# One core, two chained transformer blocks in split float32: the SBUF layout is moved so that the dense operands start at multiples of 512 bytes

## The chip, the core and the metric

The kernel runs on one core of a Trainium2 chip, in one launch. The metric is the device time of one execution in microseconds (us). Engines are named as in the profile: PE is TensorE's matrix product, PEld its weight load, DVE is VectorE, ACT is ScalarE, POOL is GpSimd, SP issues the weight DMAs. [...]

## The reference, cut to what matters

Two blocks run one after the other on 512 tokens of width 1024. Everything is float32.

```python
# block 1
h = rms_norm(x, g_pre_mix) * (1 + sc1) + sh1;  proj = h @ w_in
x = x + gt1 * rms_norm(concat(nsa_attention(...), dsa_attention(...)) @ w_out, g_post_mix)
h = rms_norm(x, g_pre_ffn) * (1 + sc2) + sh2
x = x + gt2 * rms_norm(square(relu(h @ w_up)) @ w_down, g_post_ffn)        # width 4096
# block 2
x = x + 0.5 * swiglu(rms_norm_2(x, norm_ffn1), gate, up, down)              # width 2816
p = rms_norm_2(x, norm_mix) @ w_in                                          # width 3328
x = x + concat(stick_breaking_attention(...), rwkv7_time_mix(...)) @ w_out
x = x + 0.5 * swiglu(rms_norm_2(x, norm_ffn2), gate, up, down)
```

## The kernel before

Activations lie transposed: 128 features on the partitions, 512 tokens (2048 bytes) along the row. A dense product is done in three float32r matrix products: each operand is split into a high part (float32r, rounded) and a low part (the rest), and high x high, low x high and high x low are summed in PSUM (`dense`, three calls of `mm`, whose one line is L339). The weights are the stationary operand, 128x128 (a row of 512 bytes), the activation is the moving operand, 128x512.

In the profile's rows `whi` and `wlo` are the two parts of the weights. The activations are named by what they hold: `hh`, `hl` are the normalized input of a block (pool `hp`, a pool on the right side of SBUF); `oh`, `ol` the attention's output (four tile pairs in pool `gp`, four in `hp`); `uh`, `ul` the squared ReLU in block 1's feed-forward; `vh`, `vl` the gated product in block 2's two SwiGLUs. Up products go to PSUM banks `ps_mm` (and the first ones of a SwiGLU to `ps_s`), down products to `ps_s`, so a row `ps_s<-uh,whi` is one matmul of block 1's down product.

`Stream` loads the weights: SP issues loads of 1 MB into two buffers `w32` (shown as `w`), ACT writes `whi` (L243), DVE writes `wlo` (L249), 1024 columns at a time, which is the weight of 24 matmuls. PE executes in the order in which the program lists its instructions. In the feed-forwards this order is plain: per output tile 24 matmuls over eight input tiles, one after the other. In block 2's mixer (`mix2`) the dense matmuls are fillers, listed by `weave` between the short products of the recurrence and of the attention (`ps_c`, `ps_pt`).

Where a tile lies in SBUF follows from the pools alone. Pools are stacked, from the left and from the right, and each tile takes the length of its row, rounded up to 32 bytes. So a small tile shifts all that comes behind it. In the program as built, before the change, the small constants of pool `cst` end at byte 18880 of a partition, which is 448 past a multiple of 512; `w32`, `whi`, `wlo`, the temporaries and most pools behind them start at 448 past such a multiple. In block 1's feed-forward the tile `g1` of 32 bytes lies ahead of `uh` and `ul` and moves them to 480. The right side ends 32 bytes short of a multiple of 512, which puts all tiles of `hp` at 480. `gp` happens to lie at 0.

Of the kernel before, what the change touches and what calls it, by code (L numbers as in the profile page):

```python
# [9 lines left out]
F32 = mybir.dt.float32  # L10
# [283 lines left out]
class K:  # L294
# [306 lines left out]
    def setup(self, es):  # L601
# [38 lines left out]
        cp = self.ces.enter_context(tc.tile_pool(name="cst1", bufs=1, side="right"))  # L640
# [19 lines left out]
        nc.vector.tensor_copy(cz[:, :, 0:1], self.vec("c", 0, 8).unsqueeze(2))  # L660
        self.cz = cz
        self.modc = cp.tile([128, 48], F32, name="modc")
        self.gs = cp.tile([128, 8], F32, name="gs")
        wap = self.xin.enter_context(tc.tile_pool(name="wap", bufs=1))
        self.wq = self.xin.enter_context(tc.tile_pool(name="wq", bufs=4))
        self.ada0 = deque()
# [54 lines left out]

    def open_h(self):
        self.hes = ExitStack()
        self.hp = self.hes.enter_context(self.tc.tile_pool(name="hp", bufs=8, side="right"))

    def ada_part(self, cg, bank="s"):
# [170 lines left out]
    def block1_attn(self):  # L897
# [219 lines left out]
        for i in (1, 2, 3):  # L1117
            w = work[:, WOFF[i] + 128 * i:WOFF[i] + 128 * i + 128]
            P.affine_select(out=w, in_=w, pattern=[[-1, 128]], compare_op=OP.is_ge, fill=FILL, base=0,
                            channel_multiplier=1)  # L1120
        m8 = self.ap.tile([128, 3, 8], F32, name="m8")
        dmask = self.ap.tile([128, 1152], BF, name="dmask")
        top = deque()

# [132 lines left out]
    def block1_ffn(self, oT):  # L1257
# [7 lines left out]
        es = ExitStack()  # L1265
        fp = es.enter_context(tc.tile_pool(name="fp", bufs=1))
        y = [fp.tile([128, T], F32, name=f"y{k}") for k in range(8)]
        g1 = fp.tile([128, 8], F32, name="g1")
        V.tensor_tensor(g1, self.modc[:, 16:24], self.vec("g_post_mix", 0, 8), op=OP.mult)
        self.gain("g_pre_ffn", 32)  # L1270

# [31 lines left out]
        for k in range(8):  # L1303
            t, t2 = (fp.tile([128, T], F32, name=n, tag=n, bufs=XB) for n in ("xr", "xg"))
# [492 lines left out]
    def rw_solve(self, f, u, ag):  # L1797
# [4 lines left out]
        t2 = self.rt  # L1802
# [14 lines left out]
        for half in (0, 1):  # L1817
# [9 lines left out]
            S.activation(w(ee), pv[:, :, 1], AF.Exp)  # L1827
            for _ in range(3):
                self.after("S", 256)
        dec = t2("dec", 8)  # L1830
        V.tensor_copy(dec, ch(ei)[:, :, 63])
        yield x

# [218 lines left out]
```

## Time and profile before

| | |
|---|---|
| median of three runs | 2000.85 us (1999.77 to 2000.95) |
| profiled execution, its own time | 2004.94 us |
| its span, first to last instruction | 2003.1 us |
[...]
| PE busy | 1926.2 us (96%), 11492 instructions recorded |
| DVE, ACT, POOL busy | 1079.5, 782.2, 147.8 us |
| read from HBM | 167.67 MB |

The profiled execution is 4.1 us (0.2%) above the median of the runs. Matmuls are pipelined: the duration in a row is from the first operand to the modelled end of the last result, and consecutive matmuls overlap. What a matmul costs in a stream is the distance from its start to the next start, so the rows to read are starts and counts, not durations. Some matmul records are missing from a trace.

### The profile page before, as it was taken

The page shows a single profiled execution, that of the slowest core. Times are in us where ns is not written, and L with a number is a line of the kernel's source. Part 1 is how long each engine was busy: PE and PEld are TensorE (multiplying, and loading weights), DVE is VectorE, ACT ScalarE, POOL GpSimd, SP SyncE. Part 2 cuts the span into 40 slices and gives each one's busy share as a digit, 9 for nine tenths or more (in the row PEclk, how much of TensorE's full clock was granted, in tenths as well). Part 3 has the DMA queues.
Part 4 walks back from the last instruction along what each step waited for, and adds up shares of the span by engine and source line. Part 5 has one row for each costly group of instructions (what it writes and reads, how often), then busy time and mean ns, then how long its engine had stood idle before and what let it go on. Part 6 is the DMA issues. An engine that isn't in the chain of part 4 may idle for free.

```text
span 2003.1 us, 27567 instructions
## 1 busy us (share of the span) xinstructions
PE 1926.2 (96%) x11492; PEld 1475.2 (74%) x11492; DVE 1079.5 (54%) x1798; ACT 782.2 (39%) x1353; POOL 147.8 (7%) x117
## 2 busy tenths in 40 slices
PE   5889999889999998999999999999999999999999
PEld 2766666668888886888888877677667778888887
DVE  6588875662434346543434555565657674444343
ACT  3666776442323233322222453322335652222221
POOL 3340110130000002000000000000002200000000
PEclk8999999889999998999999999999999899999999
DMA  7124123312322221223232321110101022323222
GB/s 292 56 98 143 65 87 135 106 63 84 105 84 100 90 94 61 98 84 105 85 105 85 105 92 44 43 44 23 38 18 33 1 105 84 106 85 105 87 98 90
DMA packets 27342, 171.54 MB, mean 86 GB/s; under 512 B 3153, under 2 KB 3409, under 8 KB 9041
## 3 DMA queue, kind: packets, MB, share of 16 engines
q1 hardware_dynamic: 23472, 163.44, 23.4%
q10 hardware_dynamic: 3744, 6.34, 0.9%
q8 instruction: 90, 1.47, 0.3%
q14 instruction: 36, 0.29, 0.0%
HBM read 167.67 MB, written 2.10 MB: 85 GB/s over the span
## 4 chain that ended last, share of the span: by engine, by line
PE 80%; ACT 2%; DVE 2%; POOL 1%; issue 1%; DMA 0%; ACTq 0%; POOLq 0%; DVEq 0%
PE ps_mm L339 45%; PE ps_s L339 22%; PE ps_c L339 7%; PE ps_pt L339 4%; PE ps_o L339 1%; POOL xr L1308 0%; PE ps_pt L878 0%; ACT whi L243 0%; POOL x L1357 0%; DMA x<-in_x 0%; DVE wlo L249 0%; PE ps_mm L734 0%; DVE hl L1372 0%; DVE y L1356 0%; POOL hl L1315 0%
## 5 line engine op out<-in xcount | busy, mean ns | idle before, releaser
L243 ACT ACTIVATE whi<-w 128x1024 fp32r<-128x1024 f32 (+4 forms) x277 | 274.7, 994 | 787.0 <-PE ps_mm L339 481.5
L339 PE MATMUL ps_mm<-hh,whi 128*128 128x512 f32 x1304 | 528.7, 406 | 21.7 <-ACT whi L243 9.3
L339 PE MATMUL ps_mm<-hh,wlo 128*128 128x512 f32 x1304 | 528.7, 406 | 6.1 <-DVE wlo L249 6.1
L339 PE MATMUL ps_mm<-hl,whi 128*128 128x512 f32 x1304 | 529.6, 406 | 2.9 <-DVE hl L1315 1.2
L249 DVE TENSOR_TENSOR wlo<-w,whi 128x1024 fp32r<-128x1024 f32 (+7 forms) x316 | 325.2, 1036 | 155.8 <-ACT whi L243 155.4
L339 PEld LDWEIGHTS ps_mm<-hh,whi 128*128 128x128 f32 x1304 | 248.2, 191 | 89.5 <-ACT whi L243 12.6
L339 PEld LDWEIGHTS ps_mm<-hh,wlo 128*128 128x128 f32 x1304 | 248.3, 190 | 74.7 <-DVE wlo L249 9.6
L339 PEld LDWEIGHTS ps_mm<-hl,whi 128*128 128x128 f32 x1304 | 248.1, 190 | 68.2 <-issue 4.5
L339 PE MATMUL ps_s<-vl,whi 128*128 128x512 f32 x352 | 137.2, 390 | 0.0
L339 PE MATMUL ps_s<-vh,wlo 128*128 128x512 f32 x352 | 137.0, 389 | 0.0
L339 PE MATMUL ps_s<-vh,whi 128*128 128x512 f32 x352 | 136.7, 389 | 0.0
L1413 DVE TENSOR_TENSOR su<-ps_mm,rr 128x512 f32<-128x512 f32 x42 | 29.0, 691 | 139.9 <-PE ps_mm L339 139.9
L1425 DVE SCALAR_TENSOR_TENSOR x<-ps_s,x 128x512 f32<-128x512 f32 x48 | 33.2, 692 | 129.4 <-PE ps_s L339 129.4
L339 PE MATMUL ps_s<-uh,whi 128*128 128x512 f32 x256 | 101.1, 395 | 0.0
L339 PE MATMUL ps_s<-ul,whi 128*128 128x512 f32 x256 | 101.1, 395 | 0.0
L339 PE MATMUL ps_s<-uh,wlo 128*128 128x512 f32 x256 | 101.1, 395 | 0.0
L1412 DVE TENSOR_TENSOR sg<-ps_mm,rr 128x512 f32<-128x512 f32 x42 | 29.1, 692 | 103.9 <-PE ps_mm L339 99.6
L339 PEld LDWEIGHTS ps_s<-vl,whi 128*128 128x128 f32 x352 | 66.1, 188 | 14.4 <-DVE vl L759 0.6
L339 PEld LDWEIGHTS ps_s<-vh,wlo 128*128 128x128 f32 x352 | 66.1, 188 | 13.9
L339 PEld LDWEIGHTS ps_s<-vh,whi 128*128 128x128 f32 x352 | 66.1, 188 | 13.8
L339 PEld LDWEIGHTS ps_s<-ul,whi 128*128 128x128 f32 x256 | 48.0, 187 | 11.8
L339 PEld LDWEIGHTS ps_s<-uh,whi 128*128 128x128 f32 x256 | 48.0, 187 | 11.7
(559 smaller groups left out, 2723.1 us busy)
## 6 DMA issues: line engine op xcount, KB each, us to landing
w<-in_gu SPq DMA_DIRECT2D x44, 1024.0 KB, 4.9
w<-in_win SPq DMA_DIRECT2D x17, 1024.0 KB, 5.0
w<-in_wada SPq DMA_DIRECT2D x16, 1024.0 KB, 5.4
w<-in_wup SPq DMA_DIRECT2D x16, 1024.0 KB, 4.8
w<-in_wdn SPq DMA_DIRECT2D x16, 1024.0 KB, 4.8
w<-in_dn SPq DMA_DIRECT2D x16, 1024.0 KB, 4.8
wa<-in_wada SPq DMA_DIRECT2D x8, 1024.0 KB, 13.4
w<-in_dn SPq DMA_DIRECT2D x8, 768.0 KB, 4.4
```

What stands on the lines that cost most here:

```text
L243: self.nc.scalar.activation(hi[:, :n], src, AF.Copy)
L249: self.nc.vector.tensor_tensor(lo[:, o:m], src[:, o:m], hi[:, o:m], op=OP.subtract)
L339: self.last_pe = self.nc.tensor.matmul(o, l, r, start=start, stop=stop, skip_group_check=True)
L1412: V.tensor_tensor(g, pg, r, op=OP.mult)
L1413: V.tensor_tensor(v, pu, r, op=OP.mult)
L1425: V.scalar_tensor_tensor(self.x[m], ps, 0.5, self.x[m], op0=OP.mult, op1=OP.add)
```

## The change

No instruction, no operand's shape and no order is changed; the built programs agree instruction by instruction on each engine, waits included, apart from the addresses (and the row length of three of the resized tiles). Five small edits resize or move small tiles, or add one that nothing uses.

```diff
@@ setup
-        self.gs = cp.tile([128, 8], F32, name="gs")
+        self.gs = cp.tile([128, 16], F32, name="gs")[:, :8]
@@ open_h
         self.hes = ExitStack()
+        self.hes.enter_context(self.tc.tile_pool(name="pad", bufs=1, side="right")).tile([128, 120], F32, name="pad")
         self.hp = self.hes.enter_context(self.tc.tile_pool(name="hp", bufs=8, side="right"))
@@ block1_attn
-        m8 = self.ap.tile([128, 3, 8], F32, name="m8")
+        m8 = self.ap.tile([128, 4, 8], F32, name="m8")[:, :3]
@@ block1_ffn
-        g1 = fp.tile([128, 8], F32, name="g1")
+        g1 = fp.tile([128, 128], F32, name="g1")[:, :8]
@@ rw_solve
-        dec = t2("dec", 8)
+        dec = self.small("dec", 8)
```

`dec` goes from the recurrence's pool to pool `cst`, which then ends at byte 18944 = 37 x 512; `pad` (480 bytes) fills the right end of SBUF; `g1` takes 512 bytes instead of 32. Start addresses modulo 512 bytes, and how many matmuls with 512 moving columns read them, counted in the built programs:

| operand | role | before | after | matmuls |
|---|---|---|---|---|
| `hh`, `hl` | moving | 480 | 0 | 4056 |
| `uh`, `ul` | moving | 480 | 0 | 768 |
| `oh`, `ol` in `hp` | moving | 480 | 0 | 96 |
| `oh`, `ol` in `gp` | moving | 0 | 0 | 96 |
| `vh`, `vl` | moving | 448 | 0 | 1056 |
| `whi`, `wlo` | weights of all of these | 448 | 0 | 6072 |

Other operands of PE move as well, by other amounts: the attention's `qst`, `kda`, `ksa` from 448 to 0, `kwa` from 384 to 448, `sbtri` and `negones` from 320 to 384, `P` and `PT` from 224 to 320; the token projection, where `whi` is the moving operand of 348 columns, reads half of its slices at 368 instead of 304.

## Rows read from the trace of the kernel before

**Rows 1.** The page: busy time, and the chain's shares by engine and line.

```profile
PE 1926.2 (96%) x11492; PEld 1475.2 (74%) x11492; DVE 1079.5 (54%) x1798; ACT 782.2 (39%) x1353; POOL 147.8 (7%) x117
...
PE 80%; ACT 2%; DVE 2%; POOL 1%; issue 1%; DMA 0%; ACTq 0%; POOLq 0%; DVEq 0%
```

**Rows 2.** Stretches: PE, PEld, DVE, ACT, POOL busy (instructions), granted clock, DMA share, GB/s.

```profile
32.00:120.00 88.00, 78.38 (x355) 61.37 (x355) 54.66 (x78) 51.16 (x85) 38.51 (x28) 0.90 0.21 72
120.00:320.00 200.00, 194.34 (x1199) 131.51 (x1198) 160.53 (x434) 144.43 (x366) 32.27 (x27) 1.00 0.32 111
...
425.00:769.00 344.00, 343.56 (x1473) 275.63 (x1471) 133.66 (x152) 106.39 (x137) 1.41 (x1) 1.00 0.28 95
...
876.00:1153.00 277.00, 277.00 (x1203) 225.14 (x1202) 124.08 (x147) 80.37 (x96) 0.00 (x0) 1.00 0.28 95
1153.00:1370.00 217.00, 215.36 (x2425) 155.61 (x2425) 123.73 (x244) 80.71 (x160) 0.00 (x0) 1.00 0.15 51
1370.00:1534.00 164.00, 157.94 (x1963) 112.50 (x1960) 101.02 (x206) 61.74 (x128) 3.31 (x3) 0.98 0.09 29
```

**Rows 3.** The chain that ended last, in order of time: start, length, what, count.

```profile
419.73 35.24 PE ps_mm L339 x140
454.97 44.80 PE ps_s L339 x192
499.77 44.80 PE ps_mm L339 x192
...
723.77 44.58 PE ps_s L339 x191
...
809.55 67.20 PE ps_mm L339 x288
876.75 43.55 PE ps_s L339 x192
920.30 89.60 PE ps_mm L339 x384
1009.90 43.56 PE ps_s L339 x192
...
1120.66 32.87 PE ps_s L339 x144
```

**Rows 4.** Order of time, PE, in the output projection: start, duration, instruction.

```profile
355.37 0.39 PE L339 MATMUL ps_mm<-oh,whi 128*128 128x512 f32 x1
...
358.12 0.40 PE L339 MATMUL ps_mm<-oh,whi 128*128 128x512 f32 x1
...
360.91 0.39 PE L339 MATMUL ps_mm<-oh,whi 128*128 128x512 f32 x1
```

**Rows 5.** Order of time, PE, at half clock, at the first feed-forward's start.

```profile
420.32 0.63 PE L339 MATMUL ps_mm<-hh,whi 128*128 128x512 f32 x1
420.75 0.63 PE L339 MATMUL ps_mm<-hl,whi 128*128 128x512 f32 x1
...
424.59 0.52 PE L339 MATMUL ps_mm<-hl,whi 128*128 128x512 f32 x1
```

**Rows 6.** The chain in order of time, in block 2's mixer.

```profile
1223.38 1.08 PE ps_c L339 x32
1224.46 1.13 PE ps_mm L339 x4
1225.59 1.08 PE ps_c L339 x32
```

**Rows 7.** Groups of instructions from 425 to 769 us: weight conversion on DVE and ACT.

```profile
L249 DVE TENSOR_TENSOR wlo<-w,whi 128x1024 fp32r<-128x1024 f32 x62 | 77.0, 1243 | 115.3 <-ACT whi L243 115.3
L243 ACT ACTIVATE whi<-w 128x1024 fp32r<-128x1024 f32 x62 | 65.8, 1061 | 202.3 <-PE ps_s L339 115.9 <-PE ps_mm L339 74.3 <-issue 12.0
```

**Rows 8.** The page: weight loads, KB each, median us from issue to landing.

```profile
w<-in_gu SPq DMA_DIRECT2D x44, 1024.0 KB, 4.9
```

**Rows 9.** Who waited for whom on PEld, 1153 to 1600 us: total, times, longest.

```profile
PEld ps_c L339 <- DVE tmt L1930: 11.4, 25, 1.6
PEld ps_c L339 <- DVE z L1921: 4.9, 11, 1.0
```

## The prediction

> **What bounds the kernel now.** I read the page first: PE is busy for 96% of the span and is 80% of the chain that ended last, DVE for 54% of the span, and DMA shows 0% of the chain [rows 1]. The stretches then show where PE leaves nothing free. From 425 to 769 us (block 1's feed-forward) it is busy for 343.56 of 344 us, from 876 to 1153 us (first SwiGLU) for all 277, in the mixer for 215.36 of 217 and 157.94 of 164; only the first 120 us have real gaps [rows 2]. So a matmul that ends sooner is worth its whole gain in nearly all of the span, if the next one can start sooner.
>
> The chain in order of time shows what one costs, because there the pieces are long unbroken runs. In the feed-forward a run of 192 takes 44.80 us, whether `ps_mm` (moving `hh`, `hl`) or `ps_s` (moving `uh`, `ul`). In the SwiGLU the same 192 take 43.55 or 43.56 us when they are the down product, with moving `vh`, `vl`; the up products there take 89.60 for 384, which is 44.80 for 192 again [rows 3]. So starts lie 44.80 / 192 = 233.3 ns apart in one kind and 43.56 / 192 = 226.9 ns in the other, same shape, same weights' tiles, same clock of 1.0. The kinds differ in one thing that I can name: `hh`, `hl`, `uh`, `ul` start at 480 past a multiple of 512, `vh`, `vl` at 448. The kind of product is not it, for `u` and `v` are both down products and differ, `u` and `h` are different products and agree.
>
> The output projection says the same inside one stage: its first four tile pairs lie at 0, its last four at 480. From 355.37 to 358.12 us twelve matmuls with tiles at 0 pass, 229.2 ns each; from 358.12 to 360.91 us twelve at 480, 232.5 ns each [rows 4]. The other rows that matter are those at the half clock: from 420.32 to 424.59 us ten starts, 427 ns apart, with operands at 480 [rows 5]. Halved that is 213.5 ns, so at the full clock all kinds run 13 to 20 ns over the pure rate, and at the half clock none of it is seen. I read this as the moving operand's reads, which keep up with the slow clock and not quite with the fast one, less so from a start at 480 than from 448.
>
> **The change, part by part.** The five edits have one answer: addresses. They remove no instruction and no wait. The resized tiles cost nothing themselves (`pad` is never written).
>
> *Moving operands from 480 to 0, weights from 448 to 0.* No row shows this pair. The nearest are 448 with 448 (226.9 ns), and 0 with 448 (229.2 ns). Bounds: 213.5 ns below, from the half clock, and 233.3 above, as now. I take 226.9, since 0 with 0 keeps what the SwiGLU's down product has and the output projection lacks: moving operand and weights at the same place within 512 bytes. A gain per matmul of 233.3 - 226.9 = 6.46 ns (1.24 us per 192).
>
> Now the counts. (1) The clean runs of the chain with operands at 480: in the feed-forward 140 + 6 x 192 + 191 matmuls, less some 12 of the first run, which pass at the half clock, 1471; in the two SwiGLUs 2 x (288 + 384 + 288) = 1920 (the rows of the first stand for the second). 3391 x 6.46 ns = 21.9 us. (2) The output projection: 96 at 480 gain 6.46 ns, 96 at 0 gain 229.2 - 226.9 = 2.3 ns: 0.8 us. (3) The SwiGLUs' first 192 in all, partly waiting for their inputs: 1.2 us at most, I take 1.0. (4) The mixer's 816: 5.3 us at most. There fillers stand between products of the recurrence, `ps_mm` x4 in 1.13 us after `ps_c` x32 in 1.08 us [rows 6]. A shorter filler gives time back only where the next product's operand is ready. DVE's `tmt` and `z` already end 11.4 and 4.9 us of PEld's waits there [rows 9], and these would grow by what the filler no longer covers. I take 80%, 4.2 us. (5) Block 1's first part, 360: 2.3 us at most; a clock of 0.90 until 120 us, and ACT and DVE busy for 144 and 161 of 200 us behind it [rows 2], so I take half, 1.2 us.
>
> *`vh`, `vl` from 448 to 0, with their weights:* same place relative to each other before and after, so nothing; bounds as above, 13.4 ns of gain or, if 0 with 0 acts as 0 with 448, 2.3 ns of loss, on 1056 matmuls: +2.4 us to -14.1 us.
>
> *The other PE operands* have fewer columns, or are plain float32; counted at nothing. *DVE, ACT, DMA* see new addresses as well. What covers them: a weight tile of 24 matmuls lasts 24 x 0.2333 = 5.6 us, 5.45 after; its conversion takes 1.061 us of ACT and 1.243 of DVE [rows 7], and a load lands 4.9 us after its issue [rows 8], while 1 MB lasts for two tiles, 10.9 us after. With the cover gone, a late weight would cost its own lateness per tile; here it does not come near.
>
> Sum: 21.9 + 0.8 + 1.0 + 4.2 + 1.2 = 29.1 us. The profiled execution had 2004.94 us, so one like it would take 1975.8; from the median of the runs, 2000.85, I get **1971.8 us**.
>
> [...] The rows give starts that are 233.3 ns apart at 480 and 226.9 at 448 [rows 3]. [...]
>
> **The rivals.**
>
> *A. Only half of the gain.* 0 with 0 behaves as the output projection's tiles at 0: 229.2 ns [rows 4]. Then (1) brings 3391 x 4.1 = 13.9 us, (2) 0.4, (3) to (5) 64% of 6.4, 4.1, and `vh`, `vl` lose 2.4: 1984.9 us. For it: this is the only row of a start at 0. Against: its weights lie at 448, and it alternates with tiles at 480.
>
> *B. The full rate.* A start at 0 with weights that cross no multiple of 512 removes the whole excess, 213.5 ns [rows 5]. (1) 19.8 x 3391 = 67.1 us, `vh`, `vl` 14.1, output projection 3.4, the rest three times 6.4, 19.6: 1896.6 us. Against: tiles at 0 in the output projection still take 229.2. [...]
>
> *C. No change.* The spacing comes from something that goes with the stage, such as the writes of DVE and ACT at the time, and not from the address: 2000.9 us. Against: stretches with DVE busy for 39% and 45% [rows 2] hold runs that repeat to 0.01 us, and the output projection changes its pace inside one product.
>
> *D. Slower: the two reads collide.* PE reads the moving operand and the next weights at once, and with all of them at 0 both begin at the same place, which could cost `vh`, `vl` what `h` and `u` pay now: 1056 x 6.46 = 6.8 us, with no gain elsewhere, 2007.7 us. It decides for slower once `vh`, `vl` lose over 3.8 ns (4 us) with the others unchanged. Against: at 448 with 448 they also begin at the same place, and that is the fastest row there is.
>
> **How the numbers follow.** Forecast 0.68, A 0.13, B 0.07, C 0.07, D 0.05. The likeliest case by itself spans 1966 to 1980 us: 21.9 + 0.8 alone (1978), or (3) to (5) in full (31.5 us, 1969), with 2 to 3 us on either side for stretches at the half clock that fall otherwise. The range for 8 in 10 takes in A: 1963 to 1987 us. Chances: a measurement of this kernel can tell about 0.2%, 4 us, from no change. Faster: forecast, A, B, 0.88; the same 0.07; slower 0.05.
>
> **What would show it.** In the chain, runs of 192 with `h` and `u` at 43.5 us instead of 44.80, runs of 384 at 87.1 instead of 89.60, those with `v` unchanged at 43.56. In order of time, 227 ns between all starts of the output projection at full clock. PE still busy for all of 876 to 1145 us. PEld's waits for `tmt` and `z` longer by about 1 us. At the half clock still 427 ns. I am wrong if `h` stays at 44.80 (C), if `v` slows (A or D), or if both fall under 42 us (B); and in size, if the mixer or the first 320 us don't shorten.

## The result, and the profile after

| | before | after |
|---|---|---|
| median | 2000.87 us (1999.77 to 2000.95) | 1975.22 us (1974.97 to 1976.11) |
| profiled execution, its span | 2004.94, 2003.1 us | 1976.11, 1974.3 us |
| mean granted clock, 1 being the full one | 0.978 | 0.982 |

Four runs of each; the ratio of after to before is 0.9874, 95% interval 0.9862 to 0.9886. The kernel is 25.65 us faster; 29.1 us were forecast, and 1971.8 us for the time, 3.4 us too few.

The page of the changed kernel, the lines that answer to [rows 1]:

```profile
PE 1895.1 (96%) x11492; PEld 1473.0 (75%) x11492; DVE 1079.9 (55%) x1798; ACT 781.3 (40%) x1353; POOL 147.5 (7%) x117
...
PE 79%; DVE 2%; ACT 2%; issue 1%; POOL 1%; DMA 0%; ACTq 0%; POOLq 0%; DVEq 0%
```

PE is busy for 31 us less with the same instructions; DVE and ACT, whose addresses moved too, keep their 1080 and 782 us. PE stays the bound. The first SwiGLU's stretch of the changed kernel, in the columns of [rows 2]:

```profile
866.00:1135.00 269.00, 269.00 (x1188) 222.48 (x1187) 121.60 (x145) 78.85 (x95) 0.00 (x0) 1.00 0.29 98
```

It still leaves PE nothing free (269.00 of 269). The chain of the changed kernel in order of time, the pieces that answer to [rows 3]:

```profile
418.46 34.88 PE ps_mm L339 x140
453.33 43.52 PE ps_s L339 x192
...
714.46 43.31 PE ps_s L339 x191
798.79 65.28 PE ps_mm L339 x288
864.07 43.52 PE ps_s L339 x192
907.59 87.04 PE ps_mm L339 x384
...
1103.43 32.85 PE ps_s L339 x144
...
1632.97 65.28 PE ps_mm L339 x288
```

The reader is to see one pace everywhere: 43.52 / 192 = 226.7 ns, for `h` and `u` (44.80 before) and still for `v` (43.55). In the output projection 18 matmuls now pass between these two rows, 4.08 us, 226.7 ns each, where [rows 4] had 229.2 and 232.5:

```profile
347.89 0.39 PE L339 MATMUL ps_mm<-oh,whi 128*128 128x512 f32 x1
...
351.97 0.39 PE L339 MATMUL ps_mm<-oh,whi 128*128 128x512 f32 x1
```

At half clock (0.50 granted over these 3.84 us, and over the 4.27 us of [rows 5]) nine starts still take 3.84 us, 427 ns each, as in [rows 5]:

```profile
419.05 0.63 PE L339 MATMUL ps_mm<-hh,whi 128*128 128x512 f32 x1
...
422.89 0.63 PE L339 MATMUL ps_mm<-hh,whi 128*128 128x512 f32 x1
```

One stage gained nothing. In the mixer the fillers of the changed kernel stand in the chain as in [rows 6]:

```profile
1203.35 1.08 PE ps_c L339 x32
1204.43 1.12 PE ps_mm L339 x4
1205.56 1.08 PE ps_c L339 x32
```

Four take 1.12 us, against 1.13 before. PEld's waits for `tmt` and `z` there, 1135 to 1570 us, are those of [rows 9] to the digit, so the waits did not take back any gain of the fillers:

```profile
PEld ps_c L339 <- DVE tmt L1931: 11.4, 25, 1.6
PEld ps_c L339 <- DVE z L1922: 4.9, 11, 1.0
```

### The profile page after: what moved, and what is told of

Same layout as the page of the kernel before. It is cut to its first block, busy times and chain, and to the rows that moved or that the text cites. A ratio compares the mean times of both kernels' runs of the same rounds, so it can differ in the third digit from the quotient of the medians.

```text
span 1974.3 us, 27567 instructions
## 1 busy us (share of the span) xinstructions
PE 1895.1 (96%) x11492; PEld 1473.0 (75%) x11492; DVE 1079.9 (55%) x1798; ACT 781.3 (40%) x1353; POOL 147.5 (7%) x117
## 4 chain that ended last, share of the span: by engine, by line
PE 79%; DVE 2%; ACT 2%; issue 1%; POOL 1%; DMA 0%; ACTq 0%; POOLq 0%; DVEq 0%
PE ps_mm L339 44%; PE ps_s L339 22%; PE ps_c L339 7%; PE ps_pt L339 4%; PE ps_o L339 1%; POOL xr L1309 0%; PE ps_pt L879 0%; ACT whi L243 0%; POOL x L1358 0%; DMA x<-in_x 0%; DVE wlo L249 0%; PE ps_mm L735 0%; DVE hl L1373 0%; DVE y L1357 0%; POOL hl L1316 0%
## 5 line engine op out<-in xcount | busy, mean ns | idle before, releaser
L339 PE MATMUL ps_mm<-hh,whi 128*128 128x512 f32 x1304 | 522.7, 402 | 21.3 <-ACT whi L243 9.5
L339 PE MATMUL ps_mm<-hh,wlo 128*128 128x512 f32 x1304 | 522.9, 401 | 6.1 <-DVE wlo L249 6.1
L339 PE MATMUL ps_mm<-hl,whi 128*128 128x512 f32 x1304 | 523.4, 401 | 3.9 <-DVE hl L1316 2.0
L1413 DVE TENSOR_TENSOR sg<-ps_mm,rr 128x512 f32<-128x512 f32 x42 | 29.1, 692 | 97.4 <-PE ps_mm L339 93.2
L853 ACT ACTIVATE P<-ps_s,st 128x512 f32<-128x512 f32 (+2 forms) x96 | 50.1, 528 | 15.6 <-DVE st L851 13.8
```

The lines of the kernel that those rows point to most:

```text
L339: self.last_pe = self.nc.tensor.matmul(o, l, r, start=start, stop=stop, skip_group_check=True)
L853: nc.scalar.activation(p[:, po:po + n], b[:, o:o + n], AF.Exp, bias=st[:, i:i + 1], accum_out=st[:, 4 + i:5 + i])
L1413: V.tensor_tensor(g, pg, r, op=OP.mult)
```

## The experiments

Two things were open. What of an address counts? And why did the mixer gain nothing? A row's distance below is the start of the moving operand less that of its weights, modulo 512 bytes.

**What counts.** Three theories stood behind the first four kernels. S: the place of the moving operand relative to the weights counts (the prediction's reason). L: the moving operand's own start counts. M: only starts at multiples of 512 are good. The edits are the sizes of unused or padded small tiles, all other instructions are the same.

`p1_moving448_weights448`, from the kernel before: `h`, `u`, `o` moved to the weights' 448, `v` to 0.

```diff
-        self.gs = cp.tile([128, 8], F32, name="gs")
+        self.gs = cp.tile([128, 16], F32, name="gs")[:, :8]
@@ open_h
+        ...tile_pool(name="pad", bufs=1, side="right")).tile([128, 8], F32, name="pad")
@@ block1_ffn
-        g1 = fp.tile([128, 8], F32, name="g1")
+        g1 = fp.tile([128, 128], F32, name="g1")[:, :8]
@@ swiglu
+        fp.tile([128, 16], F32, name="padv")
```

> From the kernel before: hh, hl, uh, ul and oh, ol start at 448 past a multiple of 512 like the weights, which stay at 448; vh, vl go to 0. Theory S (what counts is the place of the moving operand relative to the weights): h and u at 448 with 448 run 192 matmuls in 43.5 us as after the change, v at 0 with 448 rises to 192 x 229 ns = 44.0 us; time about 1977 us. Theory L (what counts is the moving operand's own start, a multiple of 64 bytes or not): h, u and v all at 43.5 us; about 1975 us. Theory M (only a start at a multiple of 512 gives the gain): h and u stay at 44.8 us, time 2001 us.

Measured: 1980.56 us (1975.93 to 1980.78), ratio 0.9905 (0.9888 to 0.9921), 3.6 us over the time that S gave, though the profiled run took 1975.93; what the difference is was not shown. The chain, `h` and then `v`:

```profile
495.57 43.52 PE ps_mm L339 x192
...
862.77 43.96 PE ps_s L339 x192
```

`h` at 448 with weights at 448 has the full gain, and `v`, moved to 0 with its weights left at 448, has become slower by 2.1 ns. A multiple of 512 is no merit in itself: M falls.

`p2_all480`, from the kernel before: one tile of 32 bytes in pool `cst` moves weights and `v` to 480, where `h` and `u` are already (`g1` takes 512 bytes, so that `u` stays at 480).

```diff
+        c0.tile([128, 8], F32, name="padc")
-        g1 = fp.tile([128, 8], F32, name="g1")
+        g1 = fp.tile([128, 128], F32, name="g1")[:, :8]
```

> From the kernel before: the weights, uh, ul, vh, vl all start at 480, and hh, hl stay there, so moving operand and weights are at the same place, but 32 bytes past a multiple of 64. Theory S (relative place counts): all runs of 192 take 43.5 us, time about 1976 us. Theory L (own start of the moving operand, multiple of 64): h and u stay at 44.8 us, v rises from 43.56 to 44.8 us, time about 2008 us.

Measured: 1974.94 us (1973.02 to 1976.39), ratio 0.9876 (0.9861 to 0.9890), the time of the changed kernel. The chain, `h` and `v`:

```profile
495.54 43.52 PE ps_mm L339 x192
...
862.78 43.52 PE ps_s L339 x192
```

`h` has not moved a byte and runs at 226.7 ns, because its weights have come to 480. L falls too, S stands.

`p3_h480_u448_v256_weights0` and `p4_h256_u64_v32_weights0`, from the changed kernel, weights at 0:

```diff
 p3                                                        p4
-  ...side="right")).tile([128, 120], F32, name="pad")     -  [128, 120]  +  [128, 56]
-  g1 = fp.tile([128, 128], F32, name="g1")[:, :8]         -  [128, 128]  +  [128, 16]
+  g1 = fp.tile([128, 112], F32, name="g1")[:, :8]
+  fp.tile([128, 64], F32, name="padv")                    +  [128, 8]
```

> From the changed kernel: weights at 0, hh and hl back at 480, uh and ul at 448, vh and vl at 256. Theory S: u and v, no longer at the weights' place, take 43.9 us or more per 192, h 44.8 us; about 1998 us. Theory L: h 44.8 us, u and v 43.5 us; about 1994 us.

> From the changed kernel: weights at 0, hh and hl at 256, uh and ul at 64, vh and vl at 32. Theory S: all three leave the weights' place and take 43.9 us or more per 192; about 1990 us. Theory L: h and u at multiples of 64 keep 43.5 us, v at 32 rises to 44.8 us; about 1982 us.

One run each, 2004.5 and 1981.26 us. Neither time is what S or L gave (1998 and 1994 us for the first, 1990 and 1982 for the second, where L is close though its pace for `u` is wrong), so the chains have to decide. The chain of the first, `u`, `h` and `v`:

```profile
458.86 44.80 PE ps_s L339 x192
503.66 44.80 PE ps_mm L339 x192
...
880.60 43.52 PE ps_s L339 x192
```

and of the second, `u`, `h` and `v`:

```profile
451.72 43.96 PE ps_s L339 x192
495.68 43.57 PE ps_mm L339 x192
...
865.19 44.80 PE ps_s L339 x192
```

L fails again, on `u`: a multiple of 64 both times, and 44.80 and 43.96 us. 256 is as good as 0, against S, which gave `v` in the first and `h` in the second 43.9 or more: not the place within 512 bytes counts but within 256, or less.

`p5_h128_u384_v192_weights0` and `p8_h96_u160_v320_weights0` fill in the rest (same three places: `pad` 88 and 96, `g1` 96 and 40, `padv` 48 and 80 elements).

> The changed layout with weights at 0, `h`, `o` at 128, `u` at 384, `v` at 192 past a multiple of 512. Known so far by the distance of the moving operand's start from the weights': 0 and 256 give 43.52 us per 192, 64 gives 43.96, 32, 448 and 480 give 44.80. Theory P256 (the pattern repeats every 256 bytes): `h` and `u` agree with each other, whatever their value, and `v` (192 = -64, as 448) takes 44.80. Theory P128 (it repeats every 128 bytes): `h` and `u` take 43.52, and `v` (192 = 64) takes 43.96; but then 448 = 64 should have taken 43.96 as well and did not. Theory N (no repeat: only starts close to the weights' start, on either side, collide): all three take 43.52.

> The changed layout with weights at 0, `h`, `o` at 96, `u` at 160, `v` at 320 past a multiple of 512: the distances from the weights' start that are still missing, by 32 bytes and modulo 256, and one repeat. Theory P256 (the pattern repeats every 256 bytes): `v` at 320 acts as 64 did, 43.96 us per 192. For 96 and 160 no theory gives a value; the bounds are the extremes seen, 43.52 and 44.80. Theory N (only a start close to the weights' collides) would have 160 and 320 at 43.52.

One run each, 2007.49 and 2004.6 us. The chain of the first (`u`, `h`, `v`):

```profile
455.03 44.62 PE ps_s L339 x192
499.65 44.61 PE ps_mm L339 x192
...
876.04 44.80 PE ps_s L339 x192
```

and of the second (`h` takes 44.80 in the SwiGLUs):

```profile
457.86 44.98 PE ps_s L339 x192
502.84 44.82 PE ps_mm L339 x192
...
880.42 43.96 PE ps_s L339 x192
```

The whole map, from the chains of all kernels (`p3`, `p4`, `p5` and `p8` ran once each, but within a trace the runs of 192 of one operand and stage agree within 0.05 us):

| distance | us per 192 | ns | distance + 256 | us per 192 |
|---|---|---|---|---|
| 0 | 43.52 to 43.57 | 226.7 | 256 | 43.52 to 43.57 |
| 32 | 44.80 | 233.3 | | |
| 64 | 43.96 | 229.0 | 320 | 43.96 |
| 96 | 44.80 | 233.3 | | |
| 128 | 44.62 | 232.4 | 384 | 44.62 |
| 160 | 44.98 | 234.3 | | |
| 192 | 44.80 | 233.3 | 448 | 44.80 |
| | | | 480 | 44.80 |

All four pairs that were measured agree: the pattern repeats every 256 bytes (P256). P128 and N fall with `h`, `u` at 44.6 and `v` at 44.80. 0 is the best, 64 the next, and the others lie within 0.4 us of one another.

`p11_undo_dec_and_gs` undoes two of the five edits. `dec` brings the weights back to 448. `gs` does not lie in pool `cst` but in `cst1` on the right side, and moves only the four pairs `oh`, `ol` of `gp` (in `p1`, with the larger `gs` kept, the weights stayed at 448):

```diff
-        self.gs = cp.tile([128, 16], F32, name="gs")[:, :8]
+        self.gs = cp.tile([128, 8], F32, name="gs")
-        dec = self.small("dec", 8)
+        dec = t2("dec", 8)
```

> The changed kernel with the two edits in pool `cst` undone (`gs`, `dec`), the other three kept: the weights are back at 448, `h` stays at 0, `u` and `v` are at 448, `oh`, `ol` at 0 and 32. Theory P256: only the distance modulo 256 counts, so `u` and `v` (0) keep 43.52 us per 192 and `h` (64) takes 43.96; the 704 + 1920 unbroken matmuls of `h` lose 2.29 ns each, 6.0 us, the rest under 1 us: 1981 us, range 1978 to 1984. Rival Line: a start at 0 is good in itself and the weights' place doesn't count: `h` 43.52, `u` and `v` slower than that.

Measured: 1982.97 us (1980.98 to 1985.88), ratio 0.9912 (0.9892 to 0.9932). The chain, `u` and `h`:

```profile
456.95 43.57 PE ps_s L339 x192
500.52 43.96 PE ps_mm L339 x192
```

`h` still lies at 0 and loses what a distance of 64 costs. So the place of the weights counts together with that of `h`; the rival Line falls.

`p13_lo_weights_moved_128` gives `whi` and `wlo` different distances, a gap ahead of the `wlo` buffers:

```diff
+            self.phl.tile([128, 32], F32, name="gap", bufs=1)
             lo = self.phl.tile([128, 1024], F32R, name="wlo")
-  ...tile([128, 120], F32, name="pad")
+  ...tile([128, 88], F32, name="pad")
```

> The changed kernel with a 128 byte gap between the buffers of `whi` and `wlo`, and a `pad` shorter by 128: `h`, `u`, `v`, `o` all lie at 128, `whi` at 0 (distance 128), `wlo` at 128 (distance 0). Of three matmuls (`whi` with high, `whi` with low, `wlo` with high) two have the distance 128 to their own weights and one the distance 0. Alone these took 232.4 and 226.7 ns. If the distances simply average, all runs of 192 take (2 x 232.4 + 226.7) / 3 x 192 = 44.25 us. Theory Own: the matmul's distance to its own weights counts; in order of time the start after a `wlo` matmul comes soonest. Theory Next: its distance to the weights that are loaded beside it counts; the start after the second `whi` matmul, beside which `wlo` is loaded, comes soonest. A third way is that neither shows, because starts smear over several matmuls, and only the sum of 192 can be read.

One run, 2005.56 us. The chain, `h`, whose pace `u` and `v` share (one line number further for the added line):

```profile
498.00 44.80 PE ps_mm L340 x192
```

44.80, not the 44.25 of the average, and slower than the distance 128 alone. In order of time, over some 450 matmuls of `h` of each kind in the unbroken runs, the start after a `wlo` matmul comes after 235.0 ns, those after the first and second `whi` matmul after 232.7 and 232.3. Own falls: the latest is where it expected the soonest. Next has the order right, but by 0.4 ns, where 5.7 ns lie between the distances 128 and 0 alone; it does not give the pace either. In this one layout the good distance of one of the two weights brought nothing, and whether reads meet, and which, was not shown. The run also takes a rival away: in the other kernels the temporaries behind the weights move with them, here they lie at 128 like `h`, `u` and `v`, and that helps nothing.

**Why the mixer gained nothing.** In the SwiGLUs of both layouts eight 64x64 products of a constant were put after every n matmuls of `dense`, n = 4 in the first and 12 in the second. Nobody reads their result and nothing waits for them. (`p6_cut_before` and `p7_cut_after`; the edit is the same.)

```diff
 for each of the three self.mm of dense:
+            self.cut()
...
+    def cut(self):
+        if self.ncut:
+            self.cuts += 1
+            if self.cuts % self.ncut == 0:
+                b = self.bank("pt")
+                for c in range(4):
+                    self.turn(lambda p: b[p, 64 * c:64 * c + 64], lambda p: self.ident[p, p])
```

> The layout of before; in the two SwiGLUs eight 64x64 products of a constant that nobody reads stand after every 4 matmuls (first SwiGLU) and after every 12 (second). Nothing waits for them. It is slower by the added products; it is the base for the next kernel. Theory Short bursts: groups of 4 keep a start-to-start distance above 229 ns in this layout as in the mixer. Rival Waits: the up products stand 233 ns apart within each group, the down products 227.

> The same cuts in the changed layout. Theory Short bursts (the pace at 0 with 0 is reached only from about the sixth matmul of an unbroken run; this is why the mixer gained nothing): the first SwiGLU, cut every 4, is as long as in the cut kernel of before within 1.5 us; the second, cut every 12, gains 7/12 of the full amount, 1056 x 6.46 ns x 7/12 = 4.0 us. Rival Waits (each matmul became 6.46 ns shorter in the mixer too, and waits of the recurrence took it back): nothing waits here, so both SwiGLUs gain the full 1056 x 6.46 ns = 6.8 us against the cut kernel of before.

One run each, 2410.32 and 2399.49 us. Both SwiGLUs leave PE nothing free here (600 of 600 us and 440 of 440). Order of time, PE, in the layout of before: the first matmul of a group and that of the next group, once with groups of 4, once with groups of 12:

```profile
1092.01 0.50 PE L339 MATMUL ps_mm<-hh,wlo 128*128 128x512 f32 x1
...
1093.73 0.51 PE L339 MATMUL ps_mm<-hh,whi 128*128 128x512 f32 x1
...
2128.86 0.51 PE L339 MATMUL ps_mm<-hh,whi 128*128 128x512 f32 x1
...
2132.47 0.50 PE L339 MATMUL ps_mm<-hh,whi 128*128 128x512 f32 x1
```

and in the changed layout:

```profile
1092.83 0.50 PE L339 MATMUL ps_mm<-hh,wlo 128*128 128x512 f32 x1
...
1094.58 0.50 PE L339 MATMUL ps_mm<-hh,whi 128*128 128x512 f32 x1
...
2119.83 0.50 PE L339 MATMUL ps_mm<-hh,whi 128*128 128x512 f32 x1
...
2123.39 0.50 PE L339 MATMUL ps_mm<-hh,whi 128*128 128x512 f32 x1
```

The groups of 4 shown take 1.72 us before and 1.75 after, those of 12 3.61 and 3.56. With the same matmul matched in both traces, the changed layout loses 2.3 us over the first SwiGLU (lead 10.45 us at 893, 8.13 at 1475 us), 9 ns for each of the 264 groups of `h`, and gains 2.8 over the second (8.05 at 1975, 10.83 at 2400; 4.0 were expected), 32 ns for each of 88. The mean distances between starts of `h` by place in the group tell why. The first is 337 to 339 ns in either layout. In groups of 12 the changed layout then has 231, 236, 229, 232, 230 and from the seventh on 226.6 to 227.1, while that of before stays between 228 and 235. In groups of 4 the changed layout has 235 and 236 behind the first, that of before 229 and 232. `v`, which has the distance 0 in both layouts, shows the same in both: 235 and 235 or 236 in groups of 4, under 227.1 from the seventh of 12 on. So 0 with 0 is the best place only in a run that goes on. Waits, with its 6.8 us in both, falls. Short bursts was right that groups of 4 gain nothing, but the loss lies outside the 1.5 us that it allowed, and the gain of the second SwiGLU is 1.2 us short.

The mixer itself shows the same. First and last matmul of a group of four, before and after, 0.80 and 0.82 us apart:

```profile
1224.39 0.51 PE L339 MATMUL ps_mm<-hl,whi 128*128 128x512 f32 x1
...
1225.19 0.40 PE L339 MATMUL ps_mm<-hl,whi 128*128 128x512 f32 x1
...
1206.56 0.50 PE L339 MATMUL ps_mm<-hl,whi 128*128 128x512 f32 x1
...
1207.38 0.40 PE L339 MATMUL ps_mm<-hl,whi 128*128 128x512 f32 x1
```

Of its 153 groups 91 have four matmuls. Counted from the first start to the start behind the group, the 88 of these that stand at the full clock in every trace take 100.30 us in the second profile of before (`p12_before_again`, below) and 100.83 in the changed kernel; the eight groups of ten and more take 70.22 and 69.08.

`p9_after_long_bursts` is the changed kernel with the mixer's fillers to be listed in groups of 12, `BURST` and `MINF` 12 instead of 4.

> The changed layout with the mixer's fillers listed in groups of 12 where the planner took 4 (BURST and MINF 12 instead of 4); same instructions, other order. Theory Short bursts: the bursts' first distance is 335 instead of 227 ns, and the settled pace comes after the sixth matmul; 125 more matmuls stand at a position past the fifth (752 against 627), worth 125 x 6.5 ns = 0.8 us, and some 40 bursts fewer save 40 x 0.1 us = 4 us on PE. Against it: the recurrence waits longer between its steps, and ends later, by an unknown amount; if that chain decides in the mixer, the kernel is slower than 1975 us by as much as the waits show. Expected 1972 us, range 1968 to 1985.

Measured: 1974.03 us (1970.83 to 1979.24), ratio 0.9866 (0.9833 to 0.9899). That is not told apart from the changed kernel's 1975.22. The order of the trace has 120 groups instead of 153, and 44 of four instead of 91. PE did save what was expected: between the last matmul of the first SwiGLU and the first of the second it is busy for 468.25 us instead of 474.48. But it is idle for 16.00 us instead of 10.62 (its waits for DVE's `tmt` take 5.4 us, 2.6 in the changed kernel), so the stretch shrinks from 485.11 to 484.25 us only. No version beats the changed kernel clearly.

**How much of the first profile is chance.** `p12_before_again` is the kernel before, unchanged.

> The kernel before once more, unchanged, for a second profile. Theory: its runs of 192 repeat to 0.05 us, while the stretches at half clock around the mixer's end fall otherwise than in the first profile; then the 4 us that the first pair of profiles shows there beyond the gain are this variation. Rival: the stretch of 13.65 us at half clock at the mixer's end belongs to the layout of before and comes again.

One run, 1998.78 us, span 1997.0. Its chain, the last piece of the first SwiGLU and the second's first long one:

```profile
1119.29 32.85 PE ps_s L339 x144
...
1649.16 67.20 PE ps_mm L339 x288
```

The same stretch of both profiles of before, first the one of the prediction:

```profile
1570.00:1590.00 20.00, 20.00 (x81) 13.92 (x80) 14.39 (x25) 11.81 (x23) 7.10 (x7) 0.66 0.01 2
```

and the second:

```profile
1570.00:1590.00 20.00, 20.00 (x107) 15.18 (x106) 13.33 (x25) 15.76 (x31) 7.19 (x7) 0.91 0.00 1
```

The granted clock was 0.66 there in one execution and 0.91 in the other (13.65 us at half clock against 3.41). It does not belong to the layout. Against this second profile the changed kernel is 22.7 us shorter, not 28.8.

## Why the prediction was right, and which term was not

The pace followed the addresses as forecast. The changed kernel has the pace of 448 with 448 for `h` and `u`, `v` did not slow, the half clock kept its 427 ns, and PE stayed without gaps. The price, 226.9 ns, was 226.7. That the excess over the halved 427 ns comes from reads of the moving operand that don't keep up with the fast clock was the author's reading; no run shows it.

The terms of the sum, with the second profile of before as the base where a row of the chain doesn't give them:

| term | forecast, us | measured, us | from |
|---|---|---|---|
| (1) unbroken runs | 21.9 | 22.1 | feed-forward 348.62 to 339.31, two SwiGLUs 224.00 to 217.60 each |
| (2) output projection | 0.8 | 0.5 | matched starts, 345 to 378 us |
| (3) SwiGLUs' first 192 | 1.0 | 1.0 | matched starts, 0.2 and 0.8 |
| (4) mixer's fillers | 4.2 | -0.5 | lead 15.86 us at 1152, 15.39 at 1600 us |
| (5) block 1's first part | 1.2 | 0.3 | matched starts, 120 to 320 us |

The measured terms sum to 23.4 us. The interval of the ratio allows 22.8 to 27.6, so the sum lies inside, and some 2 us of the 25.65 of the medians are placed by no row here (single executions of the kernel before lay between 1995.57 and 2009.13 us). The first 120 us are in no term: there the changed kernel lost 0.8 us against the second profile of before and gained 0.4 against the first.

Term (4) was mis-sized, and its step was the assumption that a filler "gives time back" at the rate of an unbroken run, less what waits take. The chain shows it: from the end of the first SwiGLU to the second's first long run it is 497.02 us in the second profile of before and 496.69 in the changed kernel, with the start of the second SwiGLU, 0.8 us of gain, inside. What failed was not the 80% but the 6.46 ns: fillers stand in groups of mostly four, and in such groups the changed layout is no faster (100.83 against 100.30 us). The sign that went with it, waits for `tmt` and `z` longer by about 1 us, did not come either.

The reason given, "the same place within 512 bytes", was right for the case and too narrow: the same place within 256 does as well, and it is the distance to the weights that counts. The other reading, that a start at 480 is itself worse for the moving operand than one at 448, was wrong: in `p2_all480` `h` lies at 480 and has the full pace. The rivals: A's 229 ns is what a distance of 64 costs, and the changed kernel never had it. B's 213.5 ns was reached by no distance of the map. C fell with the first run of 43.52. The loss that D feared shows at the other distances, and 0 with 0 is the best of them in a long run. A weight load does run beside a matmul (in the kernel before, the 0.19 us load for the next matmul and the 0.39 us matmul both start at 900.19 us), but whether it is two reads that collide was not shown.

The rows show up to 234.3 ns against 226.7 between starts that are all multiples of 32; why the distance counts was not shown.

## What to carry to other kernels

Where unbroken runs of float32r matmuls with 512 columns bound a kernel, read their start-to-start distance by operand, and list the start addresses of moving operand and weights: here bringing both to the same place modulo 256 bytes was worth 6.7 ns of 233, and in `p2_all480` one added tile of 32 bytes and one enlarged tile did it. Look at both, since moving one alone can lose as much (`v` in `p4`, from 0 to 32: 43.52 to 44.80 us per 192). Count only matmuls that stand in runs of more than about six (in `p7_cut_after` the pace of 226.6 to 227.1 ns came from the seventh of 12 on), and take a second profile before a few microseconds at a stage's end are put down to a change.

## What was not expected of the hardware

The pace depends on the distance between moving operand and weights with a period of 256 bytes in the four pairs measured, between 226.7 and 234.3 ns at the full clock, and not in order of distance: 64 (229.0) is better than 32 and 96 (233.3). None of it is seen at the half clock, where a start at 480 with weights at 448 and one at 0 with 0 both take 427 ns. After a switch from 64x64 products the first distance is about 337 ns in both layouts, 110 ns over the settled pace: for each filler of a group of four this is 27 ns, where no two distances of the map differ by more than 7.6. The one layout tried in which only one of the two weights has the good distance gained nothing (44.80 us per 192).
